# Seven block products for eight in three groups of q and k projections of a hybrid decoder layer

## The chip, the cores and the metric

The kernel runs on one core of one Trainium2 chip. The core has TensorE (matrix products, called PE in the profile; its weight loads are shown as PEld), VectorE (DVE), ScalarE (ACT), GpSimd (POOL) and SyncE (SP), which issues most of the transfers. Sixteen DMA engines carry these transfers. The metric is the device time of one execution in microseconds. The time before is 2951.25 us, the median of three runs.

## The reference

One decoder layer on 2048 tokens of width 1024, in float32. Cut to what matters here:

```python
h = rms_norm(x, g_attn[l]) * (1.0 + scale_a) + shift_a
proj = h @ w_in[l]
q_f, k_f, v_f, q_s, k_s, v_s, f_logit = jnp.split(proj, offsets, axis=-1)
log_f = jax.nn.log_sigmoid((f_logit + b_fgate[l]).astype(jnp.float32))
o_fox = forgetting_attention(split_heads(q_f, N_HEADS_FOX), split_heads(k_f, N_HEADS_FOX),
                             split_heads(v_f, N_HEADS_FOX), log_f.transpose(0, 2, 1))
o_sb = stick_breaking_attention(split_heads(q_s, N_HEADS_SB), split_heads(k_s, N_HEADS_SB),
                                split_heads(v_s, N_HEADS_SB))
...
x = x + gate_a * (mix @ w_out[l])
h = rms_norm(x, g_mlp[l]) * (1.0 + scale_m) + shift_m
u = causal_depthwise_conv(h @ w_up[l], conv_w[l], conv_b[l])
...
x = x + gate_m * ((jax.nn.silu(u_gate) * u_val) @ w_down[l])
```

`w_in` holds columns for q, k and v of 8 FoX heads (forgetting attention, a softmax with a decay) and of 8 stick-breaking heads, each head 64 wide.

## The kernel before

**Precision.** Every large product is made of three matmuls in a reduced float32 format: an operand is split into a high part, which ScalarE rounds, and a low part, which another engine makes by a subtraction (`split`, L44 to L46; GpSimd by default, VectorE where it is named). The terms are high x high, high x low and low x high.

**Units.** Heads are handled in pairs of 128 columns, tokens in four blocks (`tb`) of 512. The list `units` has 32 entries, ordered by kind (first `sb`, stick-breaking, then `fox`), pair and block: units 0 to 15 are stick-breaking, 16 to 31 FoX, and four units in a row share a pair. `attend` is the attention of one unit. For the stick-breaking kind it computes logits (L596, L597), two sigmoids on ScalarE (L630, L631), a mask by GpSimd (L633), a scan on VectorE (L636), then transposes (L606), a split (L610, L611) and the product with the values (L615).

**Projections** run ahead of the attention, between its steps. For one unit `proj` loads the eight tiles of h (512 KB each, L468, into the tag `hp` with ten buffers) from DRAM, where the first stick-breaking pair has stored them as high and low parts, accumulates q and then k (L342: 8 tiles x 3 matmuls of 512 columns each), and for an even pair also the values of two pairs (L413: matmuls of 256 columns). The results go to DRAM, and `load_unit` brings them back as the attention's tiles Q, K and V. `load_w` loads and splits the weights of a pair once, at block 0: tags `wraw` (raw, three buffers), `w_qk` and `w_v` (split, eight buffers each).

**Order.** The main loop over the units calls `interleave`, which takes a step of the attention, lets `follow` take as many steps of the generator `ahead` (all projections) as `pace` asks for, and takes steps of two fillers: `late_mod` (from unit 12: the late modulation vectors, with GpSimd additions at L783, and `fold_out`) and the tail's output projection. `pace` is the larger of two goals: the projection of the next unit must be done at 80% of the present one, and from unit 3 the steps are spread evenly by the weight of the units until unit 30. From unit 3 to 15 a projection step may not be issued before an attention matmul twelve back (`LAG`, `ENDQ`). SyncE issues nearly all loads and stores, in one queue.

After the attention come the output projection (L912), the MLP's up products (L1315) and down products (L1614); there, blocks of four are already multiplied with seven products for eight. The change doesn't touch these.

Of the kernel before, what the change touches and what calls it, by code (L numbers as in the profile page):

```python
# [9 lines left out]
F32 = mybir.dt.float32  # L10
# [7 lines left out]
P = 128  # L18
# [16 lines left out]
def kernel(ctx: ExitStack, tc: tile.TileContext, x, c, w_ada, b_ada, g_attn, w_in, b_fgate,  # L35
# [29 lines left out]
    qs = {}  # L65
    zs = [dram.tile([4 * NH, P], F32, name=f"zs{t}") for t in range(NTB)]
# [240 lines left out]

    def load_w(kind, p):
        base = (0 if kind == "fox" else 3 * 512) + p * P

        def load(tag, kt, first, step):
            if (kind, p) == ("sb", 0):
                raw = raws[tag][kt]
            else:
                raw = sl_.tile([P, 2, P], F32, name=f"raw_{tag}", tag="wraw", bufs=3)
                nc.sync.dma_start(raw, w_in[kt * P:(kt + 1) * P, first:first + (step + 1) * P].rearrange(
                    "p (a n) -> p a n", n=P)[:, 0:step + 1:step, :])
# [145 lines left out]
    def proj(kind, p, tb, w):  # L463
# [9 lines left out]
        yield from finish_proj(kind, p, tb, aq, w, hts)  # L473

# [335 lines left out]

    def proj_gen(u):
        kind, p, tb = u
        if tb == 0:
            weights[kind, p] = load_w(kind, p)
            results[kind, p] = []
# [4 lines left out]
    def proj_steps(u):  # L820
        kind, p, tb = u
        if (kind, p) == ("sb", 0):
            return 0 if tb == 0 else 2 * KT + 15
# [8 lines left out]
    projected = [0, 1]  # L832

    def project():
        for u in units[1:]:
# [3 lines left out]
            projected[1] += 1  # L839
# [9 lines left out]
    def pace(i):  # L849
        n = attend_steps(units[i])  # L850
        due = sum(proj_steps(u) for u in units[:i + 2])
        total = sum(proj_steps(u) for u in units)
# [10 lines left out]
    START, STOP = 3, 30  # L863

# [155 lines left out]
    weights["sb", 0], results["sb", 0] = load_w("sb", 0), []  # L1020
# [9 lines left out]
    for i, u in enumerate(units):  # L1030
# [27 lines left out]
        def follow(m):  # L1058
# [4 lines left out]
            if nxt and projected[1] > i + 1 and loaded_units[0] == i + 1:  # L1063
# [3 lines left out]
        interleave(attend(kind, p, tb, results[kind, p], Fbs), n, [(lm if i >= LATE else None, PER, False), (tail, 17 + IDLE if nxt is None else 13, True)], follow)  # L1067
# [695 lines left out]
```

## Time and profile before

| | |
|---|---|
| runs | 2954.89, 2942.51, 2951.25 us; median 2951.25 |
| profiled execution | span 2941.4 us from the first to the last instruction; no other time is given for it |
| units 0 to 2 | 0 to 234.8 us |
| units 3 to 11 (stick-breaking) | 234.8 to 686.0 us |
| units 12 to 15 (stick-breaking) | 686.0 to 882.8 us |
| units 16 to 31 (FoX) | 882.8 to 1516.9 us |
| output projection and MLP | 1516.9 to 2941.4 us |
| mean granted TensorE clock | 0.993 |

The ends of the units are the issues of their output's store (L740). The profile is that of one execution; a row of a group gives the line, the engine, the operation, the tiles written and read, the shape, the count, then the engine's busy time and the mean duration in ns of one instruction, then the engine's idle time before them and what ended it.

### The profile page before, as it was taken

The numbers are of one execution on the slowest core, as the hardware profiler recorded it, in microseconds if no ns is written. First come the engines' busy times: TensorE is split into PE (matmuls) and PEld (weight loads), VectorE is DVE, ScalarE is ACT, GpSimd is POOL, SyncE is SP. The second block draws the span as 40 slices with busy tenths as digits, with TensorE's granted clock in tenths as the row PEclk, the third lists the DMA queues.
The fourth block names the chain that finished last, engine by engine and source line by source line (L and its number), as shares of the span: only waits on it lengthen the run. The fifth ranks groups of instructions, "written<-read, shape, count | busy, mean of one in ns | idle before, by whom it ended". The sixth has DMA issues, their size and how long they took to land.

```text
span 2941.4 us, 45922 instructions
## 1 busy us (share of the span) xinstructions
PE 2867.8 (97%) x15772; PEld 2459.7 (84%) x15772; DVE 2179.5 (74%) x3464; ACT 1686.0 (57%) x3187; POOL 901.1 (31%) x967
## 2 busy tenths in 40 slices
PE   8999999999999999999999999999999999999998
PEld 7888888888988988888888788888788888888887
DVE  5787778877886656658843788888998888575476
ACT  5776767677776656658744554444444445433342
POOL 0431322243032423231213344444254543142200
PEclk8999999999999999999999999999999999999999
DMA  9749756867469794794537775554754444975644
GB/s 293 255 139 321 236 188 207 301 211 229 162 212 356 269 277 139 232 323 140 182 120 233 245 232 128 130 136 129 236 132 125 130 130 132 309 257 185 216 158 151
DMA packets 348346, 601.89 MB, mean 205 GB/s; under 512 B 34672, under 2 KB 178800, under 8 KB 348112
## 3 DMA queue, kind: packets, MB, share of 16 engines
q1 hardware_dynamic: 324208, 558.06, 57.7%
q0 software_dynamic: 10880, 20.97, 4.3%
q10 hardware_dynamic: 13024, 19.93, 1.9%
q8 instruction: 124, 2.03, 0.3%
q14 instruction: 110, 0.90, 0.1%
HBM read 420.77 MB, written 177.02 MB: 203 GB/s over the span
## 4 chain that ended last, share of the span: by engine, by line
PE 46%; DMA 3%; DVE 2%; SPq 1%; ACT 1%; issue 1%; POOL 0%; DVEq 0%; ACTq 0%; POOLq 0%
PE ps_o L1315 19%; PE ps_t L1315 7%; PE ps_o L1614 6%; PE ps_t L1614 3%; PE ps_bc L1614 3%; PE ps_o L912 1%; PE ps_pv L615 1%; DMA r<-rstd 1%; PE ps_bc L912 1%; PE ps_pt L606 1%; PE ps_o L1609 1%; DMA wo<-wos 1%; DMA hm<-hf_m 1%; SPq L895 1%; DVE op L46 1%
## 5 line engine op out<-in xcount | busy, mean ns | idle before, releaser
L1315 PE MATMUL ps_o<-op,wu 128*128 128x512 f32 x2592 | 608.0, 389 | 2.0 <-DVE snap L1366 1.5
L1315 PEld LDWEIGHTS ps_o<-op,wu 128*128 128x128 f32 x2592 | 486.2, 188 | 103.9 <-DVE snap L1366 1.9
L611 DVE TENSOR_TENSOR at<-ps_pt,at 128x512 fp32r<-128x512 f32 (+1 forms) x576 | 366.1, 652 | 100.2 <-ACT at L610 97.3
L636 DVE TENSOR_TENSOR_SCAN a<-r,a 128x512 f32<-128x512 f32 (+2 forms) x320 | 368.3, 1167 | 77.8 <-ACT a L631 39.9
L342 PE MATMUL ps_pj<-hp,w_qk 128*128 128x512 f32 x1512 | 411.2, 403 | 14.5 <-DMA hp<-hs 12.9
L610 ACT ACTIVATE at<-ps_pt 128x512 fp32r<-128x512 f32 (+1 forms) x576 | 318.5, 576 | 139.1 <-PE ps_pt L606 123.1
L615 PE MATMUL ps_pv<-at,V 128*128 128x256 f32 x2216 | 386.8, 292 | 9.3 <-DVE at L611 4.2
L615 PEld LDWEIGHTS ps_pv<-at,V 128*128 128x128 f32 x2216 | 320.9, 190 | 39.8 <-DVE at L611 11.4
L342 PEld LDWEIGHTS ps_pj<-hp,w_qk 128*128 128x128 f32 x1512 | 275.4, 190 | 71.0 <-DMA hp<-hs 16.2
L45 ACT ACTIVATE wu<-wuraw 128x512 fp32r<-128x512 f32 x204 | 128.9, 632 | 248.5 <-PE ps_o L1315 190.1
L596 PE MATMUL ps_qk<-K,Q 128*128 128x512 f32 (+2 forms) x640 | 265.7, 416 | 5.6 <-ACT a L631 3.3
L413 PE MATMUL ps_pj<-w_v,hp 128*128 128x256 f32 (+1 forms) x1536 | 236.6, 288 | 2.1 <-DVE hp L422 1.6
L597 PE MATMUL ps_qk<-K,Q 128*128 128x512 f32 (+2 forms) x640 | 235.7, 369 | 0.0
L1315 PE MATMUL ps_t<-op,wu 128*128 128x512 f32 x888 | 220.8, 390 | 1.0 <-DVE op L46 1.0
L413 PEld LDWEIGHTS ps_pj<-w_v,hp 128*128 128x128 f32 x1536 | 209.0, 189 | 10.9 <-DVE q L373 1.5
L630 ACT ACTIVATE r<-ps_qk 128x512 f32<-128x512 f32 (+2 forms) x320 | 173.1, 541 | 58.2 <-PE ps_qk L597 55.5
L46 DVE TENSOR_TENSOR wu<-wuraw,wu 128x512 fp32r<-128x512 f32 x204 | 189.6, 930 | 18.1 <-ACT wu L45 16.7
L1315 PEld LDWEIGHTS ps_t<-op,wu 128*128 128x128 f32 x888 | 166.4, 188 | 36.5 <-DVE op L46 1.8
L606 PE MATMUL ps_pt<-edge,a 128*128 128x128 f32 x1088 | 185.1, 274 | 8.4 <-DVE a L636 7.8
L1614 PE MATMUL ps_o<-op 128*128 128x512 f32 x840 | 191.5, 389 | 0.0
L1614 PEld LDWEIGHTS ps_o<-op 128*128 128x128 f32 x840 | 157.7, 188 | 32.7
L679 ACT ACTIVATE p<-p,mn 128x128 f32<-128x128 f32 (+15 forms) x128 | 153.9, 1203 | 53.3 <-DVE mn L675 52.2
(342 smaller groups left out, 5237.6 us busy)
## 6 DMA issues: line engine op xcount, KB each, us to landing
hp<-hs SPq DMA_DIRECT2D x224, 512.0 KB
wuraw<-in_w_up_dram SPq DMA_DIRECT2D x80, 512.0 KB
ra<-g SPq DMA_DIRECT2D x136, 256.0 KB
rb<-in_w_down_dram SPq DMA_DIRECT2D x108, 256.0 KB
g<-u SPq DMA_DIRECT2D x80, 256.0 KB
hs<-hp SPq DMA_DIRECT2D x32, 512.0 KB
hp<-in_w_ada_dram SPq DMA_DIRECT2D x32, 512.0 KB
qk_fox<-q SPq DMA_DIRECT2D x32, 512.0 KB
```

Of the source, the lines that this page charges most:

```text
L46: (lo_engine or nc.gpsimd).tensor_sub(lo, src, f(hi))
L342: nc.tensor.matmul(acc, w[kt][:, a, n], h[:, bb], start=kt == 0 and i == 0, stop=kt == KT - 1 and i == 2)
L413: nc.tensor.matmul(av[:, t * width:(t + 1) * width], hts[kt][:, a, tok], w[1][kt][:, bb, 0:width], start=kt == 0 and m == 0, stop=kt == KT ...
L596: nc.tensor.matmul(b[:, :cw], Q[:, hl, 0, qcols], K[:, hl, :cw], start=True, stop=False)
L597: marks.append(nc.tensor.matmul(b[:, :cw], Q[:, hl, 1, qcols], K[:, hl, :cw], start=False, stop=True).ins)
L606: nc.tensor.transpose(b[:, i * P:(i + 1) * P], blk(kts[kk], qi), ident)
L610: copies = [nc.scalar.activation(at[:, 0, lo:], b[:, lo:], AF.Copy).ins, nc.vector.tensor_sub(at[:, 1, lo:], b[:, lo:], f(at[:, 0, lo:])).ins]
L611: nc.vector.tensor_sub(at[:, 1, lo:], b[:, lo:], f(at[:, 0, lo:])).ins]
L615: m = nc.tensor.matmul(o[:, 0:2 * P], V[kt // 4][:, kt % 4, hl, :], rhs, start=first and kk == 0 and w == 0, stop=last and kk == 1 and w == 1)
L636: nc.vector.tensor_tensor_scan(rev, r[:, 0:need][:, ::-1], rev, 0.0 if right[qi] is None else right[qi][:, 0:1], ALU.mult, ALU.add)
L1315: nc.tensor.matmul(b, w[:, p, j], o[:, q], start=first and i == 0, stop=last and i == 2, skip_group_check=True)
L1614: nc.tensor.matmul(b, a[:, p, t * P:(t + 1) * P], w[:, q], start=first and i == 0, stop=last and i == 2, skip_group_check=True)
```

## The change

Four units, two pairs by two token blocks, form a group. Let h be cut in two by tokens (blocks t0 and t1) and in two by its width (top and low half), and the weight columns in q and k by the same two halves of the width. The 2 x 2 blocks are multiplied with seven products for eight, from sums and differences of the blocks of h and of the weights, and the outputs are sums of products.

Groups are FoX pairs 0 and 1, with both halves of the tokens, and FoX pairs 2 and 3 with the first half. For FoX pairs 2 and 3, blocks 2 and 3 are projected as before.

- The sums of h (`h_sums`, for all tokens) and of the weights (`w_sums`, for the four FoX pairs) are made by GpSimd and stored in DRAM, in steps of a third filler, four to a unit, from unit 3 on.
- `group` loads the operand of h of each product and, for both pairs, the operand of the weights (`w_op`: a load, a rounding, a subtraction by GpSimd), runs 12 matmuls for each pair and combines the results on VectorE and ScalarE. The value products stay plain, but load and split their weights anew for each token block (`group_values`).
- `pace` goes by new targets (`MILES`): by unit 16 the projections of unit 18's job are to be done, by unit 24 those of unit 24, by unit 30 all.
- `wraw` has two buffers for three; value tiles of the third stick-breaking pair come from the h tiles' tag. The tag `xt`, four buffers, now serves the sums too.

```diff
+    GROUPS = {("fox", 0): (0, 1), ("fox", 2): (0,)}
...
     def value_tile(p):
-        t = wide() if p == 0 else px.tile([P, D], F32, name="xt", tag="xt", bufs=4)
-        return t.rearrange("p (i n) -> p i n", n=2 * P)
+        return wide().rearrange("p (i n) -> p i n", n=2 * P)
...
+    def h_sums(t2):
+        for j in range(KT // 2):
+            def whole(half, e):
+                h = sums_tile()
+                nc.sync.dma_start(f(h), hs[2 * t2 + e][j + half * KT // 2])
+                nc.gpsimd.tensor_add(f(h)[:, 0], f(h)[:, 0], f(h)[:, 1])
+                return h
+
+            def done(i, h):
+                split(h[:, 0], h[:, 1], f(h)[:, 1])
+                nc.sync.dma_start(hsum[t2][i][j], f(h))
+
+            b12, b22, b11 = whole(0, 1), whole(1, 1), whole(0, 0)
+            yield
+            nc.gpsimd.tensor_sub(f(b22)[:, 1], f(b22)[:, 0], f(b12)[:, 0])
+            nc.gpsimd.tensor_sub(f(b12)[:, 1], f(b12)[:, 0], f(b11)[:, 0])
+            nc.gpsimd.tensor_add(f(b11)[:, 1], f(b22)[:, 1], f(b11)[:, 0])
+            done(4, b22)
+            done(3, b12)
+            yield
+            b21 = whole(1, 0)
+            nc.gpsimd.tensor_sub(f(b21)[:, 1], f(b21)[:, 0], f(b11)[:, 1])
+            done(1, b11)
+            done(6, b21)
+            yield
...
+    def w_sums(kind, p):
+        a, b = f(sums_tile()), f(sums_tile())
+        for k, t in enumerate((a, b)):
+            for half in range(2):
+                w_block(t[:, half], kind, p, k, half)
+        yield
+        nc.gpsimd.tensor_add(b[:, 1], b[:, 0], b[:, 1])
+        nc.gpsimd.tensor_sub(b[:, 0], a[:, 0], b[:, 0])
+        nc.gpsimd.tensor_sub(a[:, 0], b[:, 1], a[:, 0])
+        nc.gpsimd.tensor_sub(a[:, 1], a[:, 1], a[:, 0])
+        for i, src in ((1, a[:, 0]), (3, b[:, 1]), (4, b[:, 0]), (5, a[:, 1])):
+            nc.sync.dma_start(wsum[kind, p][i], src)
+        yield
...
+    def w_op_(kind, p, i):
+        raw = (px.tile([P, TB], F32, name="raw_op", tag="z", bufs=2) if p % 2 else
+               sl_.tile([P, TB], F32, name="raw_op", tag="wraw", bufs=2))
+        if i in wsum[kind, p]:
+            nc.sync.dma_start(raw, wsum[kind, p][i])
+        else:
+            w_block(raw, kind, p, i // 6, min(i, 1))
+        w = [sl_.tile([P, TB], F32R, name="w_op", tag="w_v", bufs=8) for _ in range(2)]
+        split(w[0], w[1], raw)
+        return w
...
+    def group(kind, p, t2):
...
+        def run(b, w, hts, first):
+            for j in range(KT // 2):
+                for n, (a, bb) in enumerate(((0, 0), (0, 1), (1, 0))):
+                    nc.tensor.matmul(b, w[a][:, j * P:(j + 1) * P], hts[j][:, bb], start=first and j == 0 and n == 0,
+                                     stop=j == KT // 2 - 1 and n == 2, skip_group_check=True)
+                if j % 2:
+                    yield
...
+        def done(e, i, b):
+            if i == 0:
+                nc.scalar.activation(tmp[e][P1], b, AF.Copy)
+            elif i == 2:
+                keep_part(e, t0, 0, b)
+            elif i == 1:
+                add(e, b, P1, T)
+            elif i == 3:
+                add(e, b, P1, W)
+            elif i == 5:
+                add(e, b, P1, P1)
+                keep_part(e, t1, 0, tmp[e][P1])
+            elif i == 4:
+                add(e, b, W, W)
+                keep_part(e, t1, 1, tmp[e][W])
+            else:
+                add(e, b, T, T)
+                keep_part(e, t0, 1, tmp[e][T])
+
+        top, low = slice(0, KT // 2), slice(KT // 2, KT)
+        for chain in ((0, 2), (1, 3, 5), (4, 6)):
+            banks = [pj(), pj()]
+            for i in chain:
+                h = load(hsum[t2][i] if i in hsum[t2] else hs[t0][top] if i == 0 else hs[t0 if i == 2 else t1][low])
+                for e, q in enumerate(ps):
+                    yield from run(banks[e], w_op(kind, q, i), h, i == chain[0])
+                    done(e, i, banks[e])
+                if i == 0:
+                    h0 = h
+            if chain[0] == 0:
+                yield from group_values(kind, p, t0, h0 + h)
+            elif chain[0] == 1:
+                yield from group_values(kind, p, t1, load(hs[t1][top]) + h)
...
-        done = sum(weight(u) for u in units[START:i])
-        span = sum(weight(u) for u in units[START:STOP])
-        base = sum(proj_steps(u) for u in units[:START + 1])
+        at = sum(weight(u) for u in units[:i])
...
-                      base + (total - base) * (done + weight(units[i]) * m / n) / span if i >= START else 0)
+                      steady(at + weight(units[i]) * m / n) if i >= START else 0)
...
     START, STOP = 3, 30
+    SUMS = 4
+    MILES = ((16, 18), (24, 24), (STOP, 31))
```

More of the change, by code (lines that the diff above doesn't have):

```diff
@@ new lines, with make_sums, need, in_row @@
+    made = set()
+    def make_sums():
+        for t2 in range(NTB // 2):
+            yield from h_sums(t2)
+            made.add(t2)
+        for kind, p in GROUPS:
+            for e in range(2):
+                yield from w_sums(kind, p + e)
+                made.add((kind, p + e))
+    sums_ahead = make_sums()
+    def need(*items):
+        while not made.issuperset(items):
+            next(sums_ahead)
+    row = {}
+    @contextmanager
+    def in_row():
+        with ExitStack() as order:
+            for ins in row.values():
+                order.enter_context(tc.issue_after(ins))
+            n = len(nc.cur_bb.bb.instructions)
+            yield
+        for ins in nc.cur_bb.bb.instructions[n:]:
+            if ins.engine in (nc.sync.engine, nc.scalar.engine):
+                row[ins.engine] = ins
```

137 lines of the change are left out of this document (124 added, 13 removed).

## The prediction

> **What bounds the kernel now.** I read the page first (engines, slices), then a table of windows by stage, then single matmuls in order of time, because a busy share of TensorE says little by itself.
>
> ```profile
> span 2941.4 us, 45922 instructions
> PE 2867.8 (97%) x15772; PEld 2459.7 (84%) x15772; DVE 2179.5 (74%) x3464; ACT 1686.0 (57%) x3187; POOL 901.1 (31%) x967
> GB/s 293 255 139 321 236 188 207 301 211 229 162 212 356 269 277 139 232 323 140 182 120 233 245 232 128 130 136 129 236 132 125 130 130 132 309 257 185 216 158 151
> ```
>
> Windows cut at the ends of units (the store of a unit's output marks it), with the columns: window, its length, busy time and instructions of PE, PEld, DVE, ACT, POOL, granted clock, DMA share and rate:
>
> ```profile
> 234.80:686.00 451.20, 440.33 (x2856) 391.25 (x2856) 358.45 (x462) 329.35 (x720) 125.83 (x158) 1.00 0.72 239
> 882.80:1324.00 441.20, 430.62 (x2798) 387.12 (x2797) 278.81 (x704) 274.22 (x528) 140.99 (x180) 0.98 0.79 266
> 1324.00:1453.70 129.70, 123.81 (x865) 107.56 (x863) 113.32 (x308) 104.52 (x198) 26.99 (x51) 1.00 0.57 180
> 2400.00:2500.00 100.00, 100.00 (x443) 82.80 (x442) 84.91 (x103) 48.12 (x67) 38.66 (x31) 1.00 0.44 126
> ```
>
> The first is units 3 to 11 (stick-breaking, with projections between the attention steps), the second the FoX units as long as projections last, the third FoX attention alone, the last a stretch of the MLP. TensorE is taken nearly everywhere at full clock, VectorE is next at 79% (358.45 of 451.20). In the MLP, 443 matmuls of 512 columns fill 100 us: 0.226 us each. So a matmul taken out is worth 0.226 us, if nothing else holds the queue up.
>
> ```profile
> L342 PE MATMUL ps_pj<-hp,w_qk 128*128 128x512 f32 x1512 | 411.2, 403 | 14.5 <-DMA hp<-hs 12.9 <-POOL hp L46 1.3 <-ACT hp L45 0.3
> 884.08 1.55 PE L342 MATMUL ps_pj<-hp,w_qk 128*128 128x512 f32 x6
> 885.47 0.82 PE L606 MATMUL ps_pt<-edge,p 128*128 128x128 f32 x6
> 888.67 1.10 PE L615 MATMUL ps_pv<-at,V 128*128 128x256 f32 x8
> ```
>
> One projection matmul lasts 403 ns on average, but six in a row end after 1.55 us: they start (1.55 - 0.39)/5 = 0.232 us apart, since they overlap in the pipeline. The same way a transpose (L606) costs (0.82 - 0.27)/5 = 0.11 us and a 256-column matmul (L615) (1.10 - 0.29)/7 = 0.116 us. The Trainium skill says in "Perfetto Trace Analysis", section "Identifying the Most-Contended Engine", that matmul busy share is a poor measure because matmuls are pipelined. By the mean duration the saving below would be 72 x 0.403 = 29.0 us; the spacing in the trace agrees with the rule and makes it 16.3 us.
>
> **What the change removes.** A plain q and k projection is 2 x 8 x 3 = 48 matmuls of 512 columns for one unit, 192 for two pairs and two token blocks. A group makes seven products of two pairs x 4 k-tiles x 3 = 24 matmuls, 168 in all. Three groups save 3 x 24 = 72 matmuls; value matmuls keep their number. **72 x 0.226 = 16.3 us off TensorE.** The upper price is the busy time of L342 divided by its count, 411.2/1512 = 0.272, that is 19.6 us. I take 16.3. h loads per group stay 32 of 512 KB (seven products x 4, and 4 loaded again for the second value block, for 4 units x 8).
>
> **What it adds: sums over units 3 to 11** (24 steps for h and 8 for weights, four to a unit, so units 3 to 10, with their last stores in 11).
>
> ```profile
> L783 POOL TENSOR_TENSOR hp<-hp 128x512 f32<-128x512 f32 x56 | 74.9, 1356 | 55.6 <-ACT hp L782 52.7 <-issue 2.8
> L45 ACT ACTIVATE hp<-hp 128x512 fp32r<-128x512 f32 x16 | 9.8, 626 | 1.7 <-DVE hp L749 1.5
> ```
>
> For each of 8 pieces of h GpSimd does 4 additions, 4 subtractions and 4 low-part subtractions, ScalarE 4 roundings. With 4 operations for each of 4 weight sets that is 96 + 16 = 112 GpSimd operations x 1.356 = 152 us and 32 x 0.626 = 20 us of ScalarE. In the 451.2 us of units 3 to 11 GpSimd goes from 125.8 to 278 us (62%), ScalarE from 329 to 349 (77%). Neither is full, so I take nothing for them directly.
>
> GpSimd slows VectorE's scan, however. Its rows for 557 to 608 us and for 608 to 686 us, and the two windows:
>
> ```profile
> 557.00:608.00 51.00, 50.00 (x305) 43.58 (x304) 40.85 (x55) 35.99 (x77) 3.45 (x10) 1.00 0.80 278
> 608.00:686.00 78.00, 73.48 (x471) 64.20 (x470) 60.23 (x74) 60.79 (x136) 41.39 (x41) 1.00 0.70 212
> ...
> L636 DVE TENSOR_TENSOR_SCAN a<-r,a 128x512 f32<-128x512 f32 x16 | 20.0, 1267 | 2.6 <-ACT a L631 1.9 <-POOL a L633 0.5
> ...
> L636 DVE TENSOR_TENSOR_SCAN a<-r,a 128x512 f32<-128x512 f32 x24 | 33.0, 1400 | 2.6 <-ACT a L631 2.3
> ...
> L636 DVE TENSOR_TENSOR_SCAN a<-r,a 128x512 f32<-128x512 f32 x135 | 178.8, 1342 | 29.6 <-ACT a L631 25.3 <-POOL a L633 2.8
> L611 DVE TENSOR_TENSOR at<-ps_pt,at 128x512 fp32r<-128x512 f32 x136 | 89.5, 677 | 27.9 <-ACT at L610 27.6
> ```
>
> GpSimd is busy 7% in the first and 53% in the second, and the scan lasts 1267 and 1400 ns: 133 ns for 46 points. The sums add 152/451 = 34 points, so 98 ns to each of the 135 scans of the stage (the row before the last): 13 us, VectorE at 371 of 451 us (82%), still under TensorE. The other end is that the two exclude each other: the scans are 178.8/451.2 = 40% of the stage, so 152 us of sums would hold VectorE up by 60 us. In the window of 608 to 686 us that would have made 41.39 x 33.0/78 = 17.5 us, and the rows show 24 x 133 ns = 3.2 us. I take the 13 us, hidden, and keep the 60 for rival 3. The Trainium skill's "SBUF — State Buffer", section "Who interferes with whom", states that exclusion, for a VectorE instruction with two SBUF inputs beside a GpSimd one that reads SBUF; by it the sum would be that of rival 3, and the trace bears out a fifth of it.
>
> **DMA is the tight place.** Per piece of h 4 loads and 4 stores of 512 KB, for 8 pieces 33.6 MB; per weight set 4 loads and 4 stores of 256 KB, for 4 sets 8.4 MB. The stage moves 451.2 us x 239 GB/s = 107.8 MB now; with 42.0 MB it is 149.8 MB, or 332 GB/s if the stage doesn't grow. The fullest 73.5-us slice of the page shows 356, unit-long windows less. SyncE's queue is in order, so a store of a sum that waits for GpSimd holds every h load, Q/K/V load and weight load behind it:
>
> ```profile
> SPq L440 <- POOL q L46: 26.5, 7, 8.6
> SPq L776 <- POOL hp L783: 23.2, 10, 5.0
> SPq L457 <- DMA vd<-xt: 25.6, 4, 9.1
> ...
> PE ps_pj L342 <- DMA hp<-hs: 12.9, 8, 6.0
> ```
>
> Such waits exist already (the first two, 7 and 10 times, up to 8.6 us; columns: total, times, longest), and yet TensorE waited for h only 8 times, 12.9 us: ten h tiles of prefetch cover them. With that cover gone, each late load is a few microseconds of an empty TensorE, since attention matmuls stand behind the waiting one. The lower end is 0, as more transfers speed nothing up; the upper end is the stage at 306 GB/s, the rate of 882.8 to 1058.9 us:
>
> ```profile
> 882.80:1058.90 176.10, 170.01 (x1075) 151.81 (x1074) 110.65 (x272) 105.66 (x205) 55.67 (x71) 0.98 0.90 306
> ```
>
> 149.8/306 = 490 us, +38. I take +8, near the lower end, because that window held 90% DMA share with TensorE busy 97% of it.
>
> **Weights in the groups.** Each group splits 14 operands of 512 columns and 2 x 8 value weights of 256; now it is 24 splits of 256 columns for two pairs, once:
>
> ```profile
> L46 POOL TENSOR_TENSOR w_qk<-raw_qk,w_qk 128x256 fp32r<-128x256 f32 x56 | 49.9, 904 | 58.7 <-ACT w_qk L45 52.9 <-PE ps_qk L597 5.7
> L45 ACT ACTIVATE w_qk<-raw_qk 128x256 fp32r<-128x256 f32 x56 | 23.2, 430 | 16.5 <-DMA raw_qk<-in_w_in_dram 9.0 <-PE ps_pj L342 6.8 <-PE ps_pt L768 0.5
> ```
>
> Three groups take 42 x 1.356 + 48 x 0.904 us of GpSimd and 12 subtractions for k that VectorE did (16), 117 us, less the 24 x 0.904 = 22 of the first two pairs' plain weights: 95 us more. ScalarE: 42 x 0.626 + 48 x 0.430 + 6 copies of 0.6 - 24 x 0.430 = 40 us more. The stretch is the 640 us from 686 to 1324, where the FoX window shows ScalarE at 62% (274.22 of 441.20) and GpSimd at 32%. Ten more VectorE additions a group, less four subtractions given to GpSimd, are 12 us of VectorE at 63%. Hidden; price without cover: rival 2. Value tiles of the third stick-breaking pair move to the h pool, and raw weights have one buffer less: nothing taken, for the queue waits 25.6 us in those four blocks now (third row above) and TensorE in none of them; at worst these four waits show, 25.6 us.
>
> **The pace.** Projections were spread by weight over units 3 to 30; now they must reach FoX unit (0, block 2) by unit 16 and stretch to unit 29. A unit of an even pair costs 48 x 0.226 + 96 x 0.116 = 22 us, of an odd one 11, a group 60; with these, the steps that fall due before unit 16 are 75% of the projection work, where 66% did (383 of 509 us for 349 of 525). Before unit 16 this is neutral: TensorE is full either way. Afterwards it is thinner, and the end matters:
>
> ```profile
> L342 PE MATMUL ps_pj<-hp,w_qk x1512: 387/393/988, 26.3 to 1324.1; 128*128 128x512 f32 x189
> ...
> L606 PE MATMUL ps_pt<-edge,p 128*128 128x128 f32 x132 | 19.7, 273 | 0.0
> L615 PE MATMUL ps_bc<-at,V 128*128 128x256 f32 x88 | 17.6, 303 | 2.5 <-ACT at L610 1.4 <-DVE at L611 1.1
> L596 PE MATMUL ps_qk<-K,Q 128*128 128x512 f32 x32 | 14.5, 454 | 0.4 <-DVE mn L675 0.3
> L597 PE MATMUL ps_qk<-K,Q 128*128 128x512 f32 x32 | 12.6, 395 | 0.0
> L615 PE MATMUL ps_pv<-at,V 128*128 128x256 f32 x56 | 9.4, 295 | 1.3 <-DVE oT L738 1.3
> ```
>
> The last projection matmul starts at 1324.1. The other rows are 1391 to 1453.7 us, attention alone. At the spacings above they need 132 x 0.11 + 144 x 0.116 + 64 x 0.23 = 46 us, some 52 with the small groups not quoted, of 62.7: 10 us are empty, where the row of busy time shows it full. From 1324 to 1453.7 I put this at 15 us. Projections that last to unit 29 would fill some of it; they also ran ahead of their pace before, and may again. Ends 0 and -15; I take -7.
>
> **Sum.** -16.3 + 8 - 7 = -15 us: span 2941.4 to 2926. The median of the runs, 2951.25, lies 10 us over the span (start and end around it, and spread of runs); it becomes **2936**.
>
> **Rivals.**
> 1. DMA becomes the bound (slower). Place: units 3 to 11. For it: 332 GB/s asked, bursts in short units (four steps also in units of 14 to 18 us). Against: the 90% window above. At 306 GB/s: 38 - 16 = +22, 2973. It decides from a rate below 149.8/467 = 321 GB/s.
> 2. Operands come late in the groups. The eight weight tiles are all held by value weights, so the next two operands pass ScalarE and GpSimd (0.63 + 1.36 = 2 us) after the value matmuls: twice a group, 12 us in all if nothing covers it. With the 8 of the sums and no gain at the end: -16 + 12 + 8 = +4, about 2955. Against: attention matmuls stand between.
> 3. GpSimd shuts the scans out. VectorE would have 358 + 60 = 418 us of work in units 3 to 11, and the two rows above wait 29.6 + 27.9 us for ScalarE: 476 us, +25, in all 25 - 16 - 7 = +2, 2953. Against: the 3.2 us measured.
> 4. The tail fills and the sums are free: -16 - 15 = -31, 2920.
> 5. The change doesn't do what it says: then the matmul count would not fall. The loops count out to 72, so no chance is kept.
>
> **Chances.** Forecast (2926 to 2945) 0.41, rival 1 0.21, rival 2 0.13, rival 3 0.07, rival 4 0.18. About 0.5%, 14.8 us, is what a measurement of this kernel can tell from no change: the lines are 2936.5 and 2966. Faster: 0.6 of the forecast's case and all of rival 4, 0.43. Slower: nearly all of rival 1, 0.20. Same: the rest, 0.37. The range 2917 to 2973 leaves out the far ends of rivals 1 and 4, 2 in 10.
>
> **What would show it.** Right: 72 matmuls of 512 columns fewer; h waits of TensorE still near 13 us; units 3 to 11 at most some 10 us longer at 320 GB/s or more; projections after 1324 minus the gain. Wrong: many h waits or a stage of 480 us (rival 1); waits of a group's matmuls for GpSimd (rival 2); scans of 1.6 us and VectorE above 90% there (rival 3).

## The result, and the profile after

| | before | after |
|---|---|---|
| median of the runs | 2950.22 us (2942.51 to 2954.89, 4 runs) | 3043.85 us (3040.2 to 3045.81, 4 runs) |
| ratio | | 1.0314, 95% interval 1.0295 to 1.0332 |
| profiled execution, span | 2941.4 us | 3041.2 us |

The changed kernel is slower by 94 us; the prediction was 15 us faster (2936 for 2951.25), and the result lies 71 us above its range. First the page of after (span, engines, GpSimd's busy tenths by slice, the two groups named here), then a row of its groups by shape:

```profile
span 3041.2 us, 46473 instructions
...
PE 2900.6 (95%) x15700; PEld 2466.6 (81%) x15700; DVE 2237.1 (74%) x3482; ACT 1731.6 (57%) x3292; POOL 1191.5 (39%) x1157
...
POOL 0474497523554334343112335444244443042200
...
L849 DVE TENSOR_TENSOR_SCAN a<-r,a 128x512 f32<-128x512 f32 (+3 forms) x320 | 420.1, 1335 | 80.0 <-ACT a L844 43.8
...
L350 PE MATMUL ps_pj<-hp,w_qk 128*128 128x512 f32 x936 | 261.0, 408 | 7.5 <-DMA hp<-hs 3.4
```

```profile
L635 PE MATMUL ps_pj<-hp,w_op 128*128 128x512 f32 x504 | 138.1, 404 | 6.1 <-DMA hp<-hsum 5.2 <-ACT w_op L45 0.8
```

The change does what it says: 936 + 504 = 1440 matmuls of 512 columns stand where 1512 stood, 72 fewer, and TensorE has 15700 matmuls for 15772. Yet it is busy 33 us longer (2900.6 against 2867.8). GpSimd is busy 290 us longer. The scan (L849, formerly L636) is still 320 instructions, but 420.1 us for 368.3.

Most of the time went in where the sums are made. Windows cut at the ends of units 2 to 11, 12 to 15 and 16 to 27, first before, then after (columns as in the prediction):

```profile
169.10:686.00 516.90, 504.42 (x3278) 448.93 (x3277) 411.61 (x533) 375.55 (x819) 149.73 (x183) 1.00 0.71 236
686.00:882.80 196.80, 188.03 (x1277) 167.95 (x1277) 155.82 (x235) 146.09 (x320) 42.66 (x65) 1.00 0.60 196
882.80:1379.40 496.60, 485.13 (x3190) 435.96 (x3189) 327.02 (x829) 317.35 (x609) 149.23 (x198) 0.99 0.76 252
```

```profile
169.00:777.80 608.80, 551.55 (x3380) 478.05 (x3378) 462.33 (x547) 399.84 (x867) 339.25 (x297) 0.96 0.84 282
777.80:981.30 203.50, 196.05 (x1268) 172.93 (x1268) 160.66 (x216) 150.75 (x332) 100.75 (x98) 1.00 0.81 277
981.30:1473.10 491.80, 459.98 (x3022) 406.38 (x3022) 333.30 (x852) 333.98 (x654) 188.67 (x243) 0.98 0.72 232
```

Units 2 to 11 are 92 us longer, units 12 to 15 7 us longer, units 16 to 27 5 us shorter; the rest of this execution is 6 us longer in work that the change doesn't touch. In the first stage TensorE idles 608.80 - 551.55 = 57.3 us where it idled 12.5, and it ran at 0.96 of its clock, which is at most 0.04 x 608.8 = 24 us. The other 23 us or so of the 92 are work: 102 more matmuls, at up to 0.226 us each. VectorE is busy 76%, GpSimd 56%, and the DMA engines 84% at 282 GB/s: none of them shows as full. What TensorE waited for in units 2 to 11, before and then after (total, times, longest):

```profile
PE ps_pt L606 <- DVE a L636: 4.4, 11, 1.0
...
PE ps_pj L342 <- DMA hp<-hs: 0.6, 1, 0.6
```

```profile
PE ps_pt L819 <- DVE a L849: 25.6, 36, 2.4
...
PE ps_pt L819 <- DVE var L937: 6.8, 2, 4.7
...
PE ps_pj L635 <- DMA hp<-hsum: 4.2, 1, 4.2
PE ps_pj L350 <- DMA hp<-hs: 2.0, 1, 2.0
```

Its waits for h are few. Over the whole execution they are 5.2 us for `hsum` and 3.4 us for `hs`, less than the 12.9 before; but 9.9 of these 12.9 stood in the FoX units, and in units 2 to 11 they went from 0.6 to 6.2. For the scan it waits 36 times there, 25.6 us for 4.4, and the longest wait of the rows, 4.7 us, is for VectorE too. And the scan itself has become slower in these units, first before, then after:

```profile
L636 DVE TENSOR_TENSOR_SCAN a<-r,a 128x512 f32<-128x512 f32 x153 | 203.4, 1347 | 32.7 <-ACT a L631 28.3 <-POOL a L633 2.8
```

```profile
L849 DVE TENSOR_TENSOR_SCAN a<-r,a 128x512 f32<-128x512 f32 x155 | 235.7, 1545 | 30.5 <-ACT a L844 27.1 <-POOL a L846 2.3
```

The mean of the 128x512 scans of the stage is 1545 ns, 198 more than before. Counted one by one in the two traces, 45 of the 153 scans before overlap an addition or subtraction of GpSimd and take 1537 ns in the mean, and the other 108 take 1267. After, 86 of 155 do and take 1769, and the other 69 take 1265. So more scans meet GpSimd, each meeting costs more, and a scan that meets none is as fast as it was. One tight place shows what lies behind the mean. At 224 to 237 us of after, the window, its scans, and GpSimd's timeline around it (start, duration):

```profile
224.00:237.00 13.00, 8.09 (x29) 6.50 (x28) 13.00 (x10) 5.90 (x15) 13.00 (x9) 0.50 0.99 371
```

```profile
L849 DVE TENSOR_TENSOR_SCAN a<-r,a 128x512 f32<-128x512 f32 x5 | 11.9, 2426 | 0.0
```

```profile
220.67 1.27 POOL L490 TENSOR_TENSOR sums<-sums 128x512 f32<-128x512 f32 x1
...
222.40 4.05 POOL L46 TENSOR_TENSOR sums<-sums 128x512 fp32r<-128x512 f32 x2
226.41 2.18 POOL L506 TENSOR_TENSOR sums<-sums 128x512 f32<-128x512 f32 x1
228.56 3.25 POOL L465 TENSOR_TENSOR hp<-hp 128x1024 f32<-128x1024 f32 x1
231.77 2.18 POOL L46 TENSOR_TENSOR sums<-sums 128x512 fp32r<-128x512 f32 x1
...
235.35 1.28 POOL L46 TENSOR_TENSOR sums<-sums 128x512 fp32r<-128x512 f32 x1
```

VectorE and GpSimd are both busy for all of the 13 us, five scans take 2426 ns each, and GpSimd's additions and subtractions, 1.27 or 1.28 us ahead of it and at its end, take 2.0 to 2.2. TensorE has 8.09 us of work and half its clock. Instruction by instruction, three scans end at 225.39, 227.53 and 229.68 us and three of GpSimd's at 224.30, 226.45 and 228.59, each some 1.1 us behind the other engine's; the scan beside the 1024-wide GpSimd instruction of 3.25 us takes 3.29. So the two take turns. Both look full, and neither is: the rows of busy time show waiting inside an instruction as work.

### The profile page after: what moved, and what is told of

It is laid out like the page before. It is cut to its first block, busy times and chain, and to the rows that moved or that the text cites. A ratio compares the mean times of both kernels' runs of the same rounds, so it can differ in the third digit from the quotient of the medians.

```text
span 3041.2 us, 46473 instructions
## 1 busy us (share of the span) xinstructions
PE 2900.6 (95%) x15700; PEld 2466.6 (81%) x15700; DVE 2237.1 (74%) x3482; ACT 1731.6 (57%) x3292; POOL 1191.5 (39%) x1157
## 5 line engine op out<-in xcount | busy, mean ns | idle before, releaser
L849 DVE TENSOR_TENSOR_SCAN a<-r,a 128x512 f32<-128x512 f32 (+3 forms) x320 | 420.1, 1335 | 80.0 <-ACT a L844 43.8
L828 PEld LDWEIGHTS ps_pv<-at,V 128*128 128x128 f32 x2216 | 327.3, 193 | 59.8 <-DVE at L824 19.5
L350 PE MATMUL ps_pj<-hp,w_qk 128*128 128x512 f32 x936 | 261.0, 408 | 7.5 <-DMA hp<-hs 3.4
L350 PEld LDWEIGHTS ps_pj<-hp,w_qk 128*128 128x128 f32 x936 | 170.0, 192 | 41.0 <-DMA hp<-hs 4.0
L819 PEld LDWEIGHTS ps_pt<-edge,a 128*128 128x128 f32 x1088 | 133.4, 144 | 70.4 <-DVE a L849 30.6
L819 PE MATMUL ps_pt<-edge,p 128*128 128x128 f32 x1088 | 170.5, 276 | 8.8 <-DVE at L824 4.6
L46 DVE TENSOR_TENSOR op<-ra,op 128x512 fp32r<-128x512 f32 x144 | 104.5, 732 | 100.8 <-ACT op L45 100.5
```

The costliest lines, as they stand in the source:

```text
L46: (lo_engine or nc.gpsimd).tensor_sub(lo, src, f(hi))
L350: nc.tensor.matmul(acc, w[kt][:, a, n], h[:, bb], start=kt == 0 and i == 0, stop=kt == KT - 1 and i == 2)
L819: nc.tensor.transpose(b[:, i * P:(i + 1) * P], blk(kts[kk], qi), ident)
L828: m = nc.tensor.matmul(o[:, 0:2 * P], V[kt // 4][:, kt % 4, hl, :], rhs, start=first and kk == 0 and w == 0, stop=last and kk == 1 and w == 1)
L849: nc.vector.tensor_tensor_scan(rev, r[:, 0:need][:, ::-1], rev, 0.0 if right[qi] is None else right[qi][:, 0:1], ALU.mult, ALU.add)
```

## The experiments

Four parts can cost the time: the new **pace**, the **groups** themselves, the sums' **transfers** and the sums' **arithmetic**. Each run is compared with the kernel before on the same chip; its median there was 2947.2 to 2950.3 us.

| run | median us (range, runs) | ratio (95% interval) |
|---|---|---|
| e1_no_sums | 2980.86 (2972.52 to 2985.69, 3) | 1.0103 (1.0049 to 1.0158) |
| e2_sums_only | 3027.43 (3026.62 to 3038.56, 3) | 1.0277 (1.0222 to 1.0332) |
| e3_sums_dma | 3004.19 (3001.19 to 3014.92, 3) | 1.0195 (1.0139 to 1.0251) |
| e4_old_pace | 3101.18 (3094.79 to 3105.03, 3) | 1.0512 (1.0459 to 1.0566) |
| e5_plain_new_pace | 2972.31 (2965.9 to 2976.6, 4) | 1.0066 (1.0046 to 1.0087) |
| e6_write_only_sums | 2996.02 (2993.13 to 3010.83, 3) | 1.016 (1.0117 to 1.0203) |
| e7_groups_no_split | 2969.78 (2960.6 to 2980.55, 8) | 1.0057 (1.0038 to 1.0075) |
| e8_held_sums | 3030.36 (3027.97 to 3039.75, 3) | 1.0271 (1.0239 to 1.0302) |
| e9_no_sums_late | 3036.2 (3026.21 to 3044.2, 3) | 1.0291 (1.0248 to 1.0334) |
| e10_plain_late | 2952.31 (2946.18 to 2958.85, 10) | 1.0011 (0.9995 to 1.0026) |
| e11_plain_transfers | 2986.81 (2986.51 to 2992.01, 3) | 1.0131 (1.0097 to 1.0166) |
| e12_plain_arithmetic | 3017.99 (3014.84 to 3018.93, 3) | 1.0229 (1.0195 to 1.0263) |
| e13_before_72_fewer | 2936.82 (2930.23 to 2939.7, 6) | 0.996 (0.9945 to 0.9975) |
| e14_new_pace_72_fewer | 2955.38 (2949.13 to 2964.05, 10) | 1.003 (1.0015 to 1.0045) |

### The sums, whole and in halves: e1, e2, e3

**e1** takes the sums out of the changed kernel; the groups load plain blocks of h and of the weights in their place.

```diff
-            nc.sync.dma_start(raw, wsum[kind, p][i])
+        w_block(raw, kind, p, i // 6, min(i, 1))
...
-                h = load(hsum[t2][i] if i in hsum[t2] else hs[t0][top] if i == 0 else hs[t0 if i == 2 else t1][low])
+                h = load(hs[t0][top] if i in (0, 1, 3) else hs[t0 if i == 2 else t1][low])
...
-(sums_ahead if i >= 3 else None, SUMS, False), 
```

> Leaves out the sums of h and of the weights; the groups load plain blocks of the same size in their place (so the products are not those of the method). Theory 1 (GpSimd's arithmetic for the sums holds the stick-breaking units up): units 2 to 11 return to about their old length and most of the 94 us goes: 2960 to 2985 us are left, the rest being thinner filling of the FoX units. Theory 2 (the sums' transfers fill the DMA queues): the same here, since the transfers go too. Theory 3 (the new pace and the groups themselves cost it): 3020 us or more.

2980.86 us: the sums cost 63 of the 94 us, and groups and pace together are still 30 us slower than before.

**e2** keeps the sums and goes back to plain projections at the old pace.

```diff
-            if tb // 2 not in GROUPS.get((kind, p // 2 * 2), ()):
+            if True:
...
-    MILES = ((16, 18), (24, 24), (STOP, 31))
+    MILES = ((STOP, 31),)
```

> Keeps the sums as work that nobody uses; all projections are plain, at the old pace. Theories 1 and 2: 70 to 95 us slower than before (3020 to 3045 us), with units 2 to 11 as slow as in the changed kernel. Theory 3: within 20 us of before.

3027.43 us: the sums alone, beside the projections of before, cost 77 us. So they need no group to do harm. (e2, e5, e10, e11 and e12 keep the changed kernel's buffers; e10, below, shows that these cost nothing that can be told from noise.)

**e3** is the changed kernel with the loads and stores of the sums but none of their arithmetic (one of its lines, the others go alike):

```diff
-                nc.gpsimd.tensor_add(f(h)[:, 0], f(h)[:, 0], f(h)[:, 1])
...
-                split(h[:, 0], h[:, 1], f(h)[:, 1])
```

> Keeps all loads and stores of the sums and the groups, but leaves out the arithmetic of the sums on GpSimd and ScalarE (what is loaded is stored). Theory 1: like the run without sums, within 15 us. Theory 2: like the changed kernel, about 3030 to 3045 us.

3004.19 us: between e1 and after, with ranges that touch neither. The transfers cost 23 us beside the groups, the arithmetic 40 more. The window of units 2 to 11 in e3 and its scans:

```profile
169.40:741.40 572.00, 540.36 (x3380) 468.19 (x3378) 423.35 (x547) 382.18 (x838) 161.25 (x185) 0.98 0.88 299
```

```profile
L839 DVE TENSOR_TENSOR_SCAN a<-r,a 128x512 f32<-128x512 f32 x155 | 207.5, 1359 | 33.3 <-ACT a L834 25.5 <-POOL a L836 6.5
```

After and e3 have the same 3380 matmuls in this stage, and it is 608.8 - 572.0 = 36.8 us longer in after. (The two profiled executions differ by only 28.0 us, since that of e3 was the slowest of its three runs; elsewhere after is 8.8 us shorter.) GpSimd is busy 178 us less in e3 (161.25 against 339.25), VectorE 39.0 us less (423.35 against 462.33), and the scan takes 1359 ns, close to the 1347 before the change. TensorE's idle time falls from 57.3 to 31.6 us, its wait for the scan from 25.6 to 12.5, and the clock rises from 0.96 to 0.98:

```profile
PE ps_pt L809 <- DVE a L839: 12.5, 26, 1.2
```

### Why GpSimd's arithmetic costs time: e6, e8, e12

Two explanations were left. Either GpSimd's reads of SBUF hold the scan up, or the sums fill GpSimd's queue and what attention needs of it (the mask, L846, which the scan waits for) comes late.

**e6** keeps GpSimd busy in the same places, but with instructions that read nothing: each of its operations becomes three fills of the tile that it wrote.

```diff
+    def blank(t):
+        for _ in range(3):
+            nc.gpsimd.memset(t, 1.0)
...
-                nc.gpsimd.tensor_add(f(h)[:, 0], f(h)[:, 0], f(h)[:, 1])
+                blank(f(h)[:, 0])
...
-                split(h[:, 0], h[:, 1], f(h)[:, 1])
+                nc.scalar.activation(h[:, 0], f(h)[:, 1], AF.Copy)
+                blank(f(h)[:, 1])
```

> The changed kernel, but each GpSimd operation of the sums is three fills of its output, which read nothing; loads, stores and ScalarE's roundings stay (so the stored sums are wrong). The sums' arithmetic was worth about 40 us (changed kernel against the run with transfers alone). Theory Q (attention's masks and weights wait in GpSimd's in-order queue behind the sums): as slow as the changed kernel, 3030 to 3050 us, if the fills keep GpSimd as busy. Theory S (GpSimd's reads hold VectorE's scans up): scans of the stick-breaking units back to about 1.3 us, and near the run with transfers alone, 3000 to 3015 us.

2996.02 us, 48 us under after and at the level of e3. Its window of units 2 to 11, its scans, its fills:

```profile
168.20:738.80 570.60, 542.87 (x3405) 472.34 (x3404) 428.21 (x548) 400.07 (x874) 314.80 (x526) 0.99 0.89 303
```

```profile
L854 DVE TENSOR_TENSOR_SCAN a<-r,a 128x512 f32<-128x512 f32 x155 | 208.6, 1362 | 31.7 <-ACT a L849 24.0 <-POOL a L851 5.8
```

```profile
L487 POOL MEMSET sums<- 128x512 f32 x336 | 162.5, 527 | 35.9 <-DMA sums<-hs 20.3 <-ACT sums L498 9.4 <-DMA sums<-in_w_in_dram 4.9
```

GpSimd is busy 314.80 of 570.6 us, 55%, as in after (56%), with 162.5 us of fills in its queue, and the scan takes 1362 ns. Of its 155 scans, 41 overlap fills and nothing else of GpSimd and take 1264 ns in the mean; the 44 that overlap nothing of it take 1270. VectorE's wait for the mask ahead of these scans (the last figure of the scan's row) is longer in e6, 5.8 us, than in after, 2.3. So a full queue is not what costs the time, and reading is. ScalarE's roundings for the sums, which e6 keeps and e3 leaves out, cost nothing that shows. The Trainium skill's "SBUF — State Buffer", section "Who interferes with whom", states just this pair: a VectorE instruction with two SBUF inputs is shut out by a GpSimd instruction that reads SBUF, and not by one that only writes it. These runs agree, at 1545 ns beside reads and 1362 ns beside fills.

**e8** holds each step of the sums behind the latest mask of the stick-breaking attention, so that a mask that has been asked for is not queued behind them.

```diff
+                for ins in amask:
+                    order.enter_context(tc.issue_after(ins))
+                if next(sums_ahead, 1) == 1:
+                    return
...
-(sums_ahead if i >= 3 else None, SUMS, False)
+(sums_held if i >= 3 else None, SUMS, False)
```

> The changed kernel, with the GpSimd instructions of each sums step queued behind the last mask of the stick-breaking attention, so that they can't be pulled ahead into unit 2. Theory B (it is their bunching that costs: GpSimd was busy 78% of unit 2 and 93% of unit 6): 15 to 40 us faster than the changed kernel. Theories Q and S with work that counts wherever it stands: within 15 us of it.

3030.36 us, 13 us under after, with intervals of the ratio that just overlap. Unit 2 of after, then of e8, and the scans of units 2 to 11 of e8:

```profile
169.00:248.60 79.60, 68.25 (x413) 59.84 (x412) 60.91 (x69) 48.37 (x103) 62.14 (x48) 0.88 0.85 296
```

```profile
169.30:234.70 65.40, 63.88 (x416) 57.56 (x415) 53.95 (x71) 46.63 (x102) 29.34 (x29) 0.97 0.76 257
...
L860 DVE TENSOR_TENSOR_SCAN a<-r,a 128x512 f32<-128x512 f32 x153 | 234.3, 1548 | 27.2 <-ACT a L854 20.9 <-POOL a L856 4.2 <-DVE a L860 0.5
```

Holding the sums back keeps them out of unit 2: GpSimd is busy 45% of it for 78%, and the unit is 14 us shorter. Over units 2 to 11 the scans stay at 1548 ns. So how the sums bunch has at most a small part in the loss, and the greater part remains with the masks let through.

**e12** has the plain projections at the old pace and the sums' arithmetic without their transfers: each load is a fill, and the stores are gone.

```diff
-                nc.sync.dma_start(f(h), hs[2 * t2 + e][j + half * KT // 2])
+                nc.gpsimd.memset(f(h), 1.0)
...
-                nc.sync.dma_start(hsum[t2][i][j], f(h))
```

> Projections plain and at the old pace, with the arithmetic of the sums on GpSimd and ScalarE alone; a fill stands for each load, nothing is stored. The sums with both cost 77 us beside plain projections, so 40 to 60 us here (2990 to 3010 us) with scans of about 1.5 us if GpSimd's reads hold the scans up whatever the queues do; under 15 us if it takes the transfers' waits too.

3017.99 us, 69 us over before and more than was expected. (GpSimd also makes the fills that stand for the loads; e6 shows fills to be nearly free.) Its window of units 2 to 11 and its scans:

```profile
169.90:754.70 584.80, 531.75 (x3258) 463.27 (x3257) 464.84 (x534) 396.78 (x857) 371.56 (x337) 0.95 0.64 211
```

```profile
L845 DVE TENSOR_TENSOR_SCAN a<-r,a 128x512 f32<-128x512 f32 x154 | 238.7, 1570 | 36.0 <-ACT a L840 31.7 <-POOL a L842 2.0
```

No DMA is added here (211 GB/s), and the scan is at 1570 ns, TensorE's idle time at 53 us and its clock at 0.95. The stage is 67.9 us longer than before's 516.9, most of the 74.9 us between the two profiled executions. Here 90 of 154 scans overlap an addition or subtraction and take 1785 ns; the other 64 take 1268.

### The transfers by themselves: e11

**e11** is e12's counterpart: plain projections, old pace, the sums' loads and stores, no arithmetic (the edits of e2 and e3 together).

```diff
-            nc.gpsimd.tensor_add(f(b11)[:, 1], f(b22)[:, 1], f(b11)[:, 0])
...
-            if tb // 2 not in GROUPS.get((kind, p // 2 * 2), ()):
+            if True:
...
-    MILES = ((16, 18), (24, 24), (STOP, 31))
+    MILES = ((STOP, 31),)
```

> Projections plain and at the old pace, with the loads and stores of the sums alone, nothing added or subtracted. Transfers were worth 23 us beside the groups: 2965 to 2980 us here. If they cost only beside the groups: within 8 us of before.

2986.81 us, 37 us over before, more than was expected. The stage:

```profile
172.00:724.30 552.30, 520.07 (x3271) 450.54 (x3270) 417.24 (x535) 374.06 (x823) 159.94 (x186) 0.99 0.87 298
```

298 GB/s against 236, and 552.3 us against 516.9; TensorE idles 32.2 us where it idled 12.5. Two of its waits in the stage:

```profile
PE ps_pt L809 <- DVE a L839: 11.1, 26, 1.1
...
PE ps_pj L350 <- DMA hp<-hs: 3.0, 3, 2.5
```

So only a small part of the new idle time is late h (3.0 us for 0.6); more of it stands at attention's own steps, such as the scan (11.1 for 4.4). How added transfers lengthen these isn't shown by these runs.

Transfers alone (37) and arithmetic alone (69) add up to more than both together in e2 (77). A likely reading, which no run tests, is that once one of them holds TensorE up, part of the other lies in the same gaps. On top of the transfers, the arithmetic costs 41 us beside plain projections (e2 less e11) and 40 beside the groups (after less e3).

### Pace and groups: e4, e5, e9, e10, e7

**e5** has neither groups nor sums and only the changed kernel's distribution of the projections (targets in units, since the plain kernel has no group jobs).

```diff
-            if tb // 2 not in GROUPS.get((kind, p // 2 * 2), ()):
+            if True:
...
-    MILES = ((16, 18), (24, 24), (STOP, 31))
+    MILES = ((16, 23), (24, 26), (STOP, 31))
...
-(sums_ahead if i >= 3 else None, SUMS, False), 
```

> No groups and no sums: all projections plain, with targets that leave the same work after units 16 and 24 as the changed kernel does (132 and 66 us). The run without sums left groups and pace at 30 us over before, 47 us over what 72 fewer matmuls should give. Theory P (thinner filling of the FoX units costs it): this kernel is as slow, 2975 to 3000 us, with some 65 us of TensorE's gaps in units 16 to 27. Theory G (the groups' own chain costs it): within 15 us of before.

2972.31 us: 22 us for the pace alone. Its three windows, to be held against the three of before:

```profile
170.20:732.70 562.50, 542.84 (x3493) 480.12 (x3492) 420.26 (x547) 379.60 (x827) 135.28 (x180) 1.00 0.70 233
732.70:937.70 205.00, 199.65 (x1262) 175.15 (x1261) 155.32 (x225) 147.21 (x325) 58.11 (x77) 1.00 0.80 266
937.70:1402.80 465.10, 445.20 (x2988) 398.64 (x2988) 320.70 (x829) 311.65 (x594) 140.51 (x190) 0.98 0.67 216
```

The two stick-breaking stages hold 200 more matmuls and are 45.6 + 8.2 = 53.8 us longer; the FoX stage holds 202 fewer and is only 31.5 us shorter. There TensorE idles 19.9 us for 11.5, at a clock of 0.98 for 0.99. In the first stages each moved matmul costs its full time (53.8 us for 200), since TensorE was nearly full; in the FoX units, thinned out, part of what is freed turns into idle time and a lower clock.

**e4** puts the changed kernel back on the old targets, **e9** gives e1 later ones, **e10** gives plain projections without sums later ones; their three new lines in this order:

```diff
-    MILES = ((16, 18), (24, 24), (STOP, 31))
+    MILES = ((STOP, 31),)
+    MILES = ((16, 16), (24, 24), (STOP, 31))
+    MILES = ((16, 17), (24, 24), (STOP, 31))
```

> The changed kernel with the old even pace from unit 3 to unit 30 in place of the new targets. Theory 3: 20 to 40 us faster than the changed kernel, in the FoX units. Theories 1 and 2: within 15 us of the changed kernel, 3030 to 3060 us.

> The run without sums, but by unit 16 only the first group must be done instead of two (60 us of projections later). Plain projections at the new pace were 22 us over before, so if early filling is what costs, this is 10 to 25 us faster than the run without sums: 2955 to 2970 us. If the groups cost it at any pace: within 8 us of 2981, or slower, as with the old pace.

> No groups, no sums; targets later than those of before: by unit 16 the projections through unit 17, by unit 24 those of unit 24 (18 and 16 steps less than before asked). If TensorE has more to fill in the FoX units than in the stick-breaking ones, it is 3 to 12 us faster than before; if the next unit's operands then come too late, slower by 5 to 20 us.

e4 loses another 57 us against after, and e9 55 us against e1; e10 is not to be told from before. So the groups need the early pace and the plain projections don't. The stretch of e9 that shows it, its window and TensorE's longest wait in it:

```profile
945.00:1062.00 117.00, 84.04 (x446) 68.40 (x445) 50.96 (x122) 52.26 (x92) 45.13 (x46) 0.83 0.79 273
```

```profile
PE ps_qk L805 <- DMA K<-qk_fox: 17.3, 1, 17.3
```

A group delivers q and k of four units at once, at its end. With later targets, attention of FoX unit (0, block 2) stands before the group that makes its K: TensorE has 84.04 us of work in 117, waits 17.3 us in one piece for K, and its mean clock there is 0.83.

**e7** is e1 with the groups' weights loaded as they come (any tile of the right shape), so that no weight of a group is rounded or subtracted. The operands also take half the buffers.

```diff
-        w = [sl_.tile([P, TB], F32R, name="w_op", tag="w_v", bufs=8) for _ in range(2)]
-        split(w[0], w[1], raw)
+        w = [sl_.tile([P, TB], F32R, name="w_op", tag="w_v", bufs=8)] * 2
+        nc.sync.dma_start(f(w[0]), hs[0][i][:, 0])
...
-                split(w[:, 0], w[:, 1], raw)
+                nc.sync.dma_start(f(w), hs[0][kt][:, :, 0:2 * P])
```

> The run without sums, and the groups' weight operands are loaded as they are instead of being split by ScalarE and GpSimd (wrong operands of the right shape; the low part is the high part's tile, so the operands take half the buffers). Theory O (operands and the split work on ScalarE and GpSimd hold the groups up): 15 to 40 us faster than the run without sums, 2940 to 2965 us. Theory P: no more than 10 us faster.

2969.78 us, 11 us under e1, though the two intervals overlap.

### What 72 matmuls are worth: e13, e14

**e13** leaves 72 matmuls out of the kernel before, **e14** out of e5: the three terms of the last tile of h, for q and k of the twelve units that the groups cover (3 x 2 x 12).

```diff
+        skip = (unit[0] == "fox" and (unit[1] < 2 or unit[2] < 2))
+        if skip and kt == KT - 1:
+            return
```

> The kernel before, with the last of eight h tiles left out of q and k in the twelve FoX units that the groups cover (six matmuls each, 72 in all, so these q and k are incomplete); loads and everything else stay. If a matmul taken out is worth its 0.226 us here: 2950 - 16 = 2934 us. If TensorE isn't what sets the end where they stand, 2942 to 2950 us.

> The same 72 matmuls left out of the plain kernel at the new pace (2972 us). If they are worth 0.226 us there: 2956 us, and the groups themselves, at 2981 us without sums, lose 25 us. If they are worth little once they stand early: 2964 to 2972 us, and the groups lose 10 to 17 us.

e13 is 0.4% faster than before (0.25 to 0.55%), 10 us by the medians and 12 by the ratio; e14 is 17 us faster than e5 by the medians, 11 by the ratios. So the matmuls are worth 10 to 17 us, at either pace. The groups of e1 compute with as few matmuls as e14 and need 25 us more (21 by the ratios), with intervals that don't overlap. This is what grouping costs beside its matmuls: about 11 may be the splitting of the weights (e1 against e7, whose intervals overlap). What the remaining 14 or so are is open; e7 against e14 (1.0057 against 1.0030) is itself near the limit of what these runs tell apart.

## Why the prediction was wrong

The chain from before to after, each link a pair of runs (links add up by construction; by the 95% intervals of the table the first is good to some 6 us, the others to some 17 to 23, so the +9 alone is not told from zero):

| link | runs | us | the prediction |
|---|---|---|---|
| pace alone | e5 less before | +22 | -7 |
| groups at that pace, matmuls saved | e1 less e5 | +9 | -16 |
| the sums' transfers | e3 less e1 | +23 | +8 |
| the sums' arithmetic | after less e3 | +40 | 0 (hidden) |
| all | | +94 | -15 |

1. **"72 x 0.226 = 16.3 us off TensorE."** The count is right, and the size too: 10 to 17 us in e13 and e14. The spacing of matmuls in time, not their mean duration (29 us), was the better price. But the groups that save these matmuls cost 21 to 25 us beside them (e1 against e14), for which the sum put nothing.
2. **"I take the 13 us, hidden."** This is the step that failed most, and it failed twice. The size: the price of GpSimd beside the scan came from one pair of windows, 133 ns for 46 points of GpSimd, and from it the judgement that the trace bears out a fifth of the exclusion. Over the stage, 178 us of reading cost VectorE 39.0 us (after against e3), three times as much and two thirds of the 60 that full exclusion was put at, and where both engines had work without a gap the scan took 2426 ns, nearly double. In the window of 608 to 686 us of before, 16 of the 24 scans did meet an addition or subtraction of GpSimd, and they took 1465 ns for 1268, so a meeting cost the scan 197 ns there; in after it cost 504. The price was read off VectorE's rows alone: in that window the additions of L783 took 1.27 to 1.31 us six times and 1.62 to 2.20 five times, so GpSimd bore part of the meetings. And the cover: VectorE at 82% "still under TensorE" was taken for room. VectorE ended at 76%, yet its 39 us came out as 37 us of a longer stage. Attention waits for each scan: the transposes need its result, TensorE's waits for it were 25.6 us in after for 12.5 in e3, its whole idle time 57.3 for 31.6, and the clock was lower as well.
3. **Rival 3** had the right mechanism, with a chance of 0.07, and the rule of the Trainium skill's "SBUF — State Buffer", section "Who interferes with whom", was right where the prediction went by its two windows. Its price of +25 us is somewhat under the 40 measured. Its sign in the profile was half wrong: scans of 1.55 us came, VectorE above 90% did not; so an engine shut out need not look full over a stage.
4. **"I take +8"** for the transfers. They cost 23 us beside the groups and 37 alone, so the other end of the bound (+38) was the better one. But it was not rival 1 as told, with many waits for h: in units 2 to 11 these rose only from 0.6 to 6.2 us in after and to 3.0 in e11. A limit of the rate is not excluded: after ran at 282 GB/s, but e11, e3 and e6 at 298, 299 and 303, close to the 306 of that bound, and e11's 37 us is close to its +38. The window with 90% DMA share that spoke for the lower end was a FoX stretch with VectorE busy 63% (110.65 of 176.10 us); the stick-breaking stage, which got the transfers, had VectorE at 80%. By which path the transfers cost what they cost stays open.
5. **The pace: "before unit 16 this is neutral".** It was not: what moves there costs its full time, 53.8 us, and comes back from the FoX units only by 31.5. The prediction gave a gain at the end, and no price for the fuller first stages or the thinned FoX units. This term was wrong by 29 us, the sign included.
6. **Weights in the groups: "Hidden".** The splits may cost about 11 us, close to the 12 of rival 2; e1 and e7 point to that but don't settle it. The wait named there isn't what shows: TensorE waited 0.8 us for a rounded weight of a group (the row of L635).
7. **The queue.** SyncE's stores behind GpSimd were named as the danger for h; the h waits stayed small over the whole execution (8.6 us for 12.9), as predicted, though in units 2 to 11 they rose to 6.2.

The sum failed because several costs were each held against the idle time of their own engine. Over units 2 to 11 VectorE shows at most 80% and GpSimd at most 64% in the runs above, and what they did to each other still lengthened it.

## What to carry to other kernels

Price a new instruction on an engine by what it does to the instructions that it meets on other engines, and take that price from the rows of both engines, in a stretch where the two run back to back. In a stage whose steps wait for one another, a lengthened link of the chain can come out nearly one for one (here 39 us of VectorE as 37 of the stage), however much idle time its engine shows. Work that is moved forward into a full stage costs all of its time there, and the stage that it leaves may give back less (here 31.5 of 53.8 us); so a saving of 16 us that needs 42 MB of traffic, 178 us of reading on GpSimd and an earlier due time must first earn these.

## What was not expected of the hardware

**Fills on GpSimd were free beside the scan.** 336 fills, 162.5 us, left the scan at 1362 ns; about as much reading brought it to 1545.

**Short waits cost clock.** The mean granted clock of before and of after:

```profile
core 0: 2941.4 us, clock 0.993
```

```profile
core 0: 3041.2 us, clock 0.983
```

In after, the window of 224 to 237 us above ran at 0.50, and TensorE's longest wait in it was 4.7 us. The records of the granted clock know only 1 and 0.5, in pieces of 3.4 us and multiples of it; up to 1.7 ms there are 5 such pieces in before, 34.1 us, and 15 in after, 92.2 us. At half speed 58 us more are at most 29 us of work lost; TensorE was busy for 79.6 of the 92.2 us and 30.8 of the 34.1, which makes it some 24 us, a quarter of the whole loss, in a kernel whose TensorE is busy 95% of the time. No long gap is needed: the piece at 354.6 us has in the 7 us before it five gaps of at most 1.7 us, the one at 989.5 us four of at most 0.56. The Trainium skill's "TensorE: Matmul & The Clock Gate", section "What's actually happening", has the same two states and a window of about 3.4 us, and the records agree with it in these; it puts an idle window ahead of the slow state, and in the record some 1.2 to 3.4 us of idle time within the last 3.4 were enough. So the waits that the table of TensorE names understate what a late scan costs.
